# The row vector g_mix of the first norm spread by eight transposes, with V's weights split chunk by chunk

## The chip, the cores and the metric

The kernel runs on one NeuronCore of one Trainium2 chip. The metric is the device time of one execution in microseconds (us); lower is better. A core has five engines that run their own instruction streams in order and wait for each other through semaphores: TensorE (PE, with its weight loads listed apart as PEld), VectorE (DVE), ScalarE (ACT), GpSimd (POOL) and SyncE (SP), from which most transfers are issued.

## The reference

One layer of an encoder for 512 positions (rows) of 1024 values. Cut to what matters here:

```python
def rms_norm(x, g):
    y = x * lax.rsqrt(jnp.mean(jnp.square(x), axis=-1, keepdims=True) + 1e-6)
    return y * g

u = rms_norm(x, g_mix)                 # x: 512 x 1024, g_mix: 1024
z = u @ w_in                           # w_in: 1024 x 4360; columns q, k, v of two branches, f, gates
y_a = sliding_window_attention(q_a, k_a, v_a, sinks) @ w_br_swa
y_b = forgetting_attention(q_b, k_b, v_b, f_b + b_forget) @ w_br_fox
g0, g1 = sigmoid(gate_logits)
h = x + (g0 * y_a + g1 * y_b) @ w_mix_out
h = h + square(relu(rms_norm(h, g_mlp) @ w_ff1)) @ w_ff2
h = h + sigmoid(rms_norm(h, g_ple) @ w_ple_gate) * (p @ w_ple_proj)
out = rms_norm(h, g_final)
```

The change concerns the first two lines alone: the first norm, and the product of its result with the 648 columns of w_in that hold V of both branches and the forget logits.

## The kernel before

**Tiling.** The 512 rows are four blocks of 128 (`tb` 0 to 3), the 1024 columns eight chunks of 128 (`k` 0 to 7). Every product is made three times with operands cut in a high and a low part: ACT writes the high part (a cast), DVE the low one (the difference), and PE adds high x high, high x low and low x high.

**The first stage (lines 403 to 520).** For a block `tb`, `square1` (lines 432 and 439 on ACT, 435 on DVE for block 0's second half) makes sums of squares, `rms_rstd` (lines 359 and 362, POOL) the reciprocal root `n_rs`, and `scale1` (line 447, DVE) two scaled halves `n_xn` of 128 x 512, multiplied by `g_bc`, the vector g_mix repeated on all 128 partitions. `to_uT` transposes the eight chunks on PE (line 379, `n_tr`, four chunks to a PSUM tile), and `hi_lo` cuts them in `u` high (line 70, ACT) and low (line 71, DVE). `split_v(k)` cuts the chunk's rows of V's weights, `wv`, into `wv_h` (line 452, ACT) and `wv_l` (line 453, DVE). `v_mm(tb, k, nk)` (line 466) takes the chunks into the two accumulators `va` and `vb`: for nk chunks first u high x wv_h, then u high x wv_l, then u low x wv_h, each as a pair of matmuls of 320 and 328 columns.

**Where g_bc comes from.** `g_row` is loaded as one row on one partition; two matmuls with a row of ones (line 494) repeat it on all partitions in two PSUM tiles `g_ps`, and ACT copies them to `g_bc` (line 501). PE runs 16 transposes of the identity before (line 490, `warm`) and 14 behind (line 498), whose results nobody reads.

**The order.** In this stage the order on PE, POOL, ACT, DVE and SP is the one in which the code is written (`manual_schedule`). Block 0: scale, `split_v` 0 and 1, both halves of `to_uT`, `split_v` 2 and 3, `v_mm` of the chunk pairs 0-1 and 2-3, squares of block 1, `split_v` 4 and 5, scale of block 1, `split_v` 6 and 7, `v_mm` 4-5, transposes of block 1, `v_mm` 6-7. Blocks 1 to 3 follow chunk by chunk.

**The transfers.** SP issues them in the order x block 0 (two halves, `g_row` between them), `wv` for chunks 0-1 and 2-3, x block 1, `wv` 4-5, `wv` 6-7, x blocks 2 and 3. `wv` has three buffers, so that `wv` 6-7 is issued when DVE has done `wv_l` of chunk 1.

Of the kernel before, what the change touches and what calls it, by code (L numbers as in the profile page):

```python
# [8 lines left out]
F32 = mybir.dt.float32  # L9
# [5 lines left out]
P = 128  # L15
S = 512
D = 1024
NT = S // P
KT = D // P
# [4 lines left out]
EPS = 1e-6  # L24
C_QA, C_KA, C_VA, C_QB, C_KB, C_VB, C_F, C_G = 0, 512, 640, 768, 1280, 1792, 2304, 2312

N_WARM = 16
N_WARM2 = 14
N_PIECES = 4
N_PRE = 4  # L30
SWA_ACT = (0, 1)
# [19 lines left out]
def layer_kernel(ctx: ExitStack, tc: tile.TileContext, x, p, g_mix, w_in, b_forget, swa_sinks,  # L51
# [318 lines left out]
                                           ALU.mult)  # L370
        return xn

    def to_uT(xn, uh, ul, tb, trp, name, tg="tr"):

        for half in range(2):
            tr = trp.tile([P, 4, P], F32, tag=tg, bufs=3, name=f"{name}_tr{half}")
            for j in range(4):
                k = half * 4 + j
                nc.tensor.transpose(tr[:, j, :], xn[:, k * P:(k + 1) * P], ident)
            sl = (slice(None), slice(half * 4, half * 4 + 4), slice(tb * P, (tb + 1) * P))  # L380
            hi_lo(uh[sl], ul[sl], tr)
# [21 lines left out]
    s0_st = ExitStack()  # L403
    s0 = s0_st.enter_context(tc.tile_pool(name="s0", bufs=1))
    g_bc = s0.tile([P, D], F32, name="g_mix_bc")
    g_row = s0.tile([1, D], F32, name="g_row")
    ones_row = s0.tile([1, P], F32, name="ones_row")
    nc.vector.memset(ones_row, 1.0)
    wv_h = s0.tile([P, KT, 648], F32R, name="wv_h")
    wv_l = s0.tile([P, KT, 648], F32R, name="wv_l")  # L410
    xts, wvs, xn1 = [], [], {}
# [1 line left out]
    def load_x(tb):  # L413
        xt = s0.tile([P, D], F32, tag="xt", bufs=3, name=f"x_{tb}")
        for half in range(2):
            if tb == 0 and half == 1:
                nc.sync.dma_start(g_row, g_mix)
            sl = slice(half * 512, half * 512 + 512)
            nc.sync.dma_start(xt[:, sl], x[tb * P:(tb + 1) * P, sl])
        xts.append(xt)  # L420

    def load_wv(k):
# [6 lines left out]
    def square1(tb):  # L429
        acc = sm.tile([P, 2], F32, tag="acc1", name=f"acc1_{tb}")  # L430
        xn = xn1[tb] = s0.tile([P, D], F32, tag="xn", bufs=2, name=f"n1_{tb}_xn")
        nc.scalar.activation(xn[:, 0:512], xts[tb][:, 0:512], AF.Square, scale=1.0 / 32,
                             accum_out=acc[:, 0:1])
        if tb == 0:
            nc.vector.tensor_tensor_reduce(out=xn[:, 512:], in0=xts[tb][:, 512:],
                                           in1=xts[tb][:, 512:], scale=1.0 / D, scalar=0.0,
                                           op0=ALU.mult, op1=ALU.add, accum_out=acc[:, 1:2])
        else:
            nc.scalar.activation(xn[:, 512:], xts[tb][:, 512:], AF.Square, scale=1.0 / 32,
                                 accum_out=acc[:, 1:2])  # L440
        return acc

    def scale1(tb, acc):
        rs = rms_rstd(acc, f"n1_{tb}")
        for half in range(2):
            sl = slice(half * 512, half * 512 + 512)
            nc.vector.scalar_tensor_tensor(xn1[tb][:, sl], xts[tb][:, sl], rs, g_bc[:, sl],
                                           ALU.mult, ALU.mult)

    def split_v(k):  # L450
# [24 lines left out]

    with tc.manual_schedule(engines={ET.Activation, ET.DVE, ET.SP}):
        load_x(0)
        load_wv(0)
        load_wv(2)
        load_x(1)  # L480
        load_wv(4)
        load_wv(6)
        load_x(2)
        load_x(3)
        bcast_row(bf_bc, b_forget[0])
        bcast_row(sink_bc, swa_sinks[0])

        warm = psA.tile([P, 4, P], F32, tag="tr", bufs=3, name="warm")
        for j in range(N_WARM):
            nc.tensor.transpose(warm[:, j % 4, :], ident, ident)  # L490
        gps = []
        for half in range(2):
            ps = psA.tile([P, S], F32, tag="sc", bufs=3, name=f"g_ps{half}")
            nc.tensor.matmul(ps, ones_row, g_row[:, half * 512:half * 512 + 512], start=True,
                             stop=True)
            gps.append(ps)
        for j in range(N_WARM2):
            nc.tensor.transpose(warm[:, j % 4, :], ident, ident)
        acc = square1(0)
        for half in range(2):  # L500
            nc.scalar.copy(g_bc[:, half * 512:half * 512 + 512], gps[half])
        scale1(0, acc)
        split_v(0)
        split_v(1)
        to_uT(xn1[0], uh, ul, 0, psA, "n1_0")
        split_v(2)
        split_v(3)
        v_mm(0, 0, 2)
        v_mm(0, 2, 2)
        acc = square1(1)  # L510
        split_v(4)
        split_v(5)
        scale1(1, acc)
        split_v(6)
        split_v(7)
        v_mm(0, 4, 2)
        to_uT(xn1[1], uh, ul, 1, psA, "n1_1")
        v_mm(0, 6, 2)
        for tb in range(1, NT):
            if tb < NT - 1:  # L520
                acc = square1(tb + 1)
                scale1(tb + 1, acc)
            v_out(tb - 1)
            for k in range(KT):
                v_mm(tb, k)
                if k == 4 and tb < NT - 1:
                    to_uT(xn1[tb + 1], uh, ul, tb + 1, psA, f"n1_{tb + 1}")
            if tb == 2:
                unit("ka")
        v_out(NT - 1)  # L530
# [948 lines left out]
```

## Time and profile before

| | |
|---|---|
| median of 3 runs | 721.81 us (720.74 to 724.39) |
| the profiled execution | 720.46 us, of which the span from first to last instruction is 718.7 us |
| granted TensorE clock, mean | 0.995 |
| PE / DVE / ACT busy | 706.7 us (98%) / 530.8 us (74%) / 449.8 us (63%) |
| the first V matmul | starts at 10.10 us |

A row of the timeline gives the start in us from the start of the span, the time taken in us, the engine, the line, the operation, the tiles written and read, the count of instructions that were merged in the row, and in brackets how long the engine was idle before it and what ended that. Matmuls overlap, so that a single PE row is longer than the distance to the next one.

### The profile page before, as it was taken

Reading aid. Unit: us, or ns where it says so; the run is one execution under the profiler, and the core shown is the slowest. Engines: PE = TensorE matmul, PEld = TensorE weight load, DVE = VectorE, ACT = ScalarE, POOL = GpSimd, SP = SyncE. Lnnn points to the kernel's source line nnn. Section 1 sums busy time; section 2 is a strip of 40 time slices with the busy share of each in tenths; the row PEclk is TensorE's granted clock in tenths of the full one; section 3 lists DMA queues with packets and bytes.
Section 4 is the critical chain, followed back from the end, with each engine's and each line's share of the span. In section 5 each row is a group of like instructions: output and inputs, shape, how many; then the busy total and the mean of one; then the engine's idle time right before and its main releaser. Section 6 shows DMA issues by size and latency. Waiting matters only on the chain.

```text
span 718.7 us, 11465 instructions
## 1 busy us (share of the span) xinstructions
PE 706.7 (98%) x4234; PEld 627.1 (87%) x4234; DVE 530.8 (74%) x898; ACT 449.8 (63%) x838; POOL 86.5 (12%) x127
## 2 busy tenths in 40 slices
PE   9999999999999999999999999999999999999995
PEld 7988888888888998888899889988999899988884
DVE  6557888877696556545879985899579966997564
ACT  6547888779853553344777636874578546866452
POOL 1011211100001200002410102010300020010101
PEclk9999999999999999999999999999999999999998
DMA  9256456670364894450995599749995689079002
GB/s 279 76 163 159 116 123 157 153 192 1 118 210 112 157 347 153 159 174 8 256 216 203 107 287 171 232 87 262 184 255 117 159 231 227 31 147 352 0 30 88
DMA packets 74041, 116.72 MB, mean 162 GB/s; under 512 B 6657, under 2 KB 44033, under 8 KB 73986
## 3 DMA queue, kind: packets, MB, share of 16 engines
q1 hardware_dynamic: 65922, 86.64, 38.1%
q0 software_dynamic: 8064, 29.36, 22.1%
q8 instruction: 33, 0.54, 0.3%
q14 instruction: 22, 0.18, 0.1%
HBM read 72.93 MB, written 4.19 MB: 107 GB/s over the span
## 4 chain that ended last, share of the span: by engine, by line
PE 89%; DVE 6%; ACT 2%; DMA 1%; issue 1%; POOL 0%; POOLq 0%; DVEq 0%; ACTq 0%
PE pf L74 5%; PE pf L76 5%; PE pf L75 5%; PE s_6x L1295 3%; PE s_4x L1295 3%; PE s_2x L1295 3%; PE s_0x L1295 3%; PE h_sc L738 2%; PE h_pv L808 2%; PE h_tr L796 2%; PE psm L76 2%; PE psm L74 2%; PE psy L74 2%; PE psy L75 2%; PE psm L75 2%; PE psy L76 2%
## 5 line engine op out<-in xcount | busy, mean ns | idle before, releaser
L298 POOL DMA_DIRECT2D wq<-wq x26 | 23.6, 943 | 173.5 <-DVE u154l L325 25.9
L756 ACT ACTIVATE s<-s,h_nm 128x128 f32<-128x128 f32 (+1 forms) x64 | 32.6, 512 | 5.9 <-DVE h_nm L749 5.2
L71 DVE TENSOR_TENSOR h_ptl<-h_tr,h_pth 128x512 fp32r<-128x512 f32 (+2 forms) x40 | 22.9, 604 | 4.0 <-ACT h_pth L70 3.6
L359 POOL TENSOR_SCALAR n_ms<-acc 128x1 f32<-128x1 f32 x15 | 5.2, 344 | 165.3 <-ACT junk L1061 100.3
L70 ACT CAST h_pth<-h_tr 128x512 fp32r<-128x512 f32 (+2 forms) x40 | 19.5, 523 | 1.8 <-PE h_tr L796 1.4
L70 ACT CAST u<-n_tr 128x512 fp32r<-128x512 f32 x22 | 12.1, 585 | 13.1 <-PE n_tr L1109 5.8
L466 PE MATMUL va<-wv_h,u 128*128 128x320 f32 x64 | 19.9, 316 | 0.2 <-ACT u L70 0.2
L796 PE MATMUL h_tr<-ident,s 128*128 128x128 f32 x136 | 19.6, 277 | 0.2
L466 PE MATMUL vb<-wv_h,u 128*128 128x328 f32 x64 | 19.5, 313 | 0.0
L298 POOL DMA_DIRECT2D wgw<-wgw x8 | 7.1, 971 | 101.7 <-DVE u25l L325 77.7
L71 DVE TENSOR_TENSOR u<-n_tr,u 128x512 fp32r<-128x512 f32 x22 | 14.5, 684 | 6.2 <-ACT u L70 6.2
L1061 ACT ACTIVATE junk<-h_sb 128x512 f32<-128x512 f32 x16 | 10.1, 630 | 12.3 <-DVE h_sb L1051 9.8
L808 PE MATMUL h_pv<-h_ptl,v 128*128 128x256 f32 (+1 forms) x64 | 16.9, 305 | 0.4 <-DVE h_ptl L71 0.3
L808 PE MATMUL h_pv<-h_pth,v 128*128 128x256 f32 (+1 forms) x64 | 17.3, 291 | 0.0
L796 PEld LDWEIGHTS h_tr<-ident,s 128*128 128x128 f32 x136 | 15.0, 141 | 2.0 <-ACT s L776 0.5
L1385 DVE TENSOR_TENSOR sgp<-sgp,pp 128x512 f32<-128x512 f32 (+1 forms) x9 | 5.7, 633 | 14.8 <-ACT sgp L1384 14.8
L1051 DVE TENSOR_TENSOR h_sb<-psm,h_sb 128x512 f32<-128x512 f32 x8 | 5.5, 689 | 14.3 <-PE psm L76 14.3
L776 ACT ACTIVATE s<-s,h_rec 128x128 f32<-128x128 f32 (+2 forms) x32 | 14.2, 482 | 2.4 <-DVE h_rec L770 2.4
L818 DVE TENSOR_TENSOR h_ao<-h_pv,h_ao 64x512 f32<-64x512 f32 x16 | 10.9, 681 | 6.0 <-ACT h_ao L817 5.8
L744 DVE CUSTOM_DVE_ANT_0 s<-h_sc,causal 128x128 f32<-128x128 f32 (+3 forms) x32 | 13.8, 483 | 0.3 <-PE h_sc L738 0.3
L770 DVE RECIPROCAL h_rec<-h_den 128x4 f32<-128x4 f32 x16 | 3.0, 185 | 14.5 <-ACT s L756 14.3
L808 PEld LDWEIGHTS h_pv<-h_ptl,v 128*128 128x128 f32 x64 | 12.1, 188 | 1.7 <-DVE h_ptl L71 0.8
(1606 smaller groups left out, 2775.4 us busy)
## 6 DMA issues: line engine op xcount, KB each, us to landing
wq<-in_w_ff_dram SPq DMA_DIRECT2D x45, 512.0 KB, 4.9
wq<-wq POOLq DMA_DIRECT2D x26, 512.0 KB, 5.5
wq_c<-in_w_ff_dram SPq DMA_DIRECT2D x9, 512.0 KB, 6.0
wg<-in_w_in_dram SPq DMA_DIRECT2D x4, 1024.0 KB, 5.3
wgw<-in_w_in_dram SPq DMA_DIRECT2D x8, 512.0 KB, 4.8
wgw<-wgw POOLq DMA_DIRECT2D x8, 512.0 KB, 5.8
wmix<-in_w_mix_out_dram SPq DMA_DIRECT2D x4, 1024.0 KB, 5.1
wpg<-in_w_ple_gate_dram SPq DMA_DIRECT2D x4, 1024.0 KB, 8.4
```

The source lines that it names most:

```text
L70: nc.scalar.copy(hi, src)
L71: nc.vector.tensor_tensor(lo, src, hi.bitcast(F32), ALU.subtract)
L74: nc.tensor.matmul(ps, lh, rh, start=start, stop=False)
L75: nc.tensor.matmul(ps, lh, rl, start=False, stop=False)
L76: nc.tensor.matmul(ps, ll, rh, start=False, stop=stop)
L298: nc.gpsimd.dma_start(q, other, accum_op=ALU.add)
L466: nc.tensor.matmul(ps, u[:, kk_, ts_], w[:, kk_, c0:c1], start=kk_ == 0 and n == 0, stop=kk_ == KT - 1 and n == 2)
L738: nc.tensor.matmul(ps[:, off:off + n], qs[i][z][:, qb * P:(qb + 1) * P], kk[i][z][:, k0:k0 + n], start=z == 0, stop=z == 1)
L756: nc.scalar.activation(sl, sl, AF.Exp, bias=nm[:, qb:qb + 1], accum_out=den[:, qb:qb + 1])
L796: nc.tensor.transpose(tr[:, n, :], c["s"][:, o, :], ident)
L808: nc.tensor.matmul(pv[:, q0:q0 + nq, :], V2[kb][:, c["v"], :], t[:, o:o + nq, :], start=n == 0, stop=n == 2 * NT - 1, skip_group_check=True)
L1295: nc.tensor.matmul(ps, o[:, j, ts_], w[:, j, :], start=tg != "" and j == 0 and n == 0, stop=j == 1 and n == 2, skip_group_check=True)
```

## The change

`g_row` is loaded as 8 rows of 128 instead of 1 row of 1024, and one transpose turns it into 8 columns `g_col`, which DVE copies out of PSUM. Eight transposes, each of one column read 128 times, then fill the two PSUM tiles `g_ps`. Block 0's scaling reads these PSUM tiles, and the copies to `g_bc` stand behind it. The idle transposes number 10, 4 and 6 in three places. The second half of x block 0 is issued by ACT. In block 0, `split_v` goes chunk by chunk, `to_uT` in two halves with V matmuls between, `v_mm` takes one chunk at a time, and the scaling of block 1 stands ahead of `split_v` 4 to 7.

```diff
-N_WARM = 16
-N_WARM2 = 14
+N_WARM = (10, 4, 6)
...
-    def to_uT(xn, uh, ul, tb, trp, name, tg="tr"):
+    def to_uT(xn, uh, ul, tb, trp, name, tg="tr", halves=(0, 1)):
-        for half in range(2):
+        for half in halves:
...
-    g_row = s0.tile([1, D], F32, name="g_row")
-    ones_row = s0.tile([1, P], F32, name="ones_row")
-    nc.vector.memset(ones_row, 1.0)
+    g_row = s0.tile([KT, P], F32, name="g_row")
+    g_col = s0.tile([P, KT], F32, name="g_col")
...
-            if tb == 0 and half == 1:
-                nc.sync.dma_start(g_row, g_mix)
             sl = slice(half * 512, half * 512 + 512)
-            nc.sync.dma_start(xt[:, sl], x[tb * P:(tb + 1) * P, sl])
+            queue = nc.scalar if tb == 0 and half == 1 else nc.sync
+            queue.dma_start(xt[:, sl], x[tb * P:(tb + 1) * P, sl])
+            if tb == 0 and half == 0:
+                nc.sync.dma_start(g_row, g_mix[0].rearrange("(k q) -> k q", q=P))
...
-            nc.vector.scalar_tensor_tensor(xn1[tb][:, sl], xts[tb][:, sl], rs, g_bc[:, sl],
+            nc.vector.scalar_tensor_tensor(xn1[tb][:, sl], xts[tb][:, sl], rs,
+                                           gps[half] if tb == 0 else g_bc[:, sl],
                                            ALU.mult, ALU.mult)
...
-        for j in range(N_WARM):
-            nc.tensor.transpose(warm[:, j % 4, :], ident, ident)
+        def warm_up(n):
+            for j in range(n):
+                nc.tensor.transpose(warm[:, j % 4, :], ident, ident)
+        warm_up(N_WARM[0])
+        ps = psA.tile([P, KT], F32, tag="mm", bufs=2, name="g_colps")
+        nc.tensor.transpose(ps, g_row, ident[0:KT, 0:KT])
+        nc.vector.tensor_copy(g_col, ps)
+        warm_up(N_WARM[1])
         gps = []
         for half in range(2):
             ps = psA.tile([P, S], F32, tag="sc", bufs=3, name=f"g_ps{half}")
-            nc.tensor.matmul(ps, ones_row, g_row[:, half * 512:half * 512 + 512], start=True,
-                             stop=True)
+            for j in range(4):
+                k = half * 4 + j
+                nc.tensor.transpose(ps[:, j * P:(j + 1) * P],
+                                    g_col[:, k:k + 1].to_broadcast([P, P]), ident)
             gps.append(ps)
-        for j in range(N_WARM2):
-            nc.tensor.transpose(warm[:, j % 4, :], ident, ident)
+        warm_up(N_WARM[2])
         acc = square1(0)
+        scale1(0, acc)
         for half in range(2):
             nc.scalar.copy(g_bc[:, half * 512:half * 512 + 512], gps[half])
-        scale1(0, acc)
         split_v(0)
-        split_v(1)
-        to_uT(xn1[0], uh, ul, 0, psA, "n1_0")
-        split_v(2)
-        split_v(3)
-        v_mm(0, 0, 2)
-        v_mm(0, 2, 2)
+        to_uT(xn1[0], uh, ul, 0, psA, "n1_0", halves=(0,))
+        v_mm(0, 0)
+        for k in (1, 2, 3):
+            split_v(k)
+            if k == 1:
+                v_mm(0, 1)
+        to_uT(xn1[0], uh, ul, 0, psA, "n1_0", halves=(1,))
+        v_mm(0, 2)
+        v_mm(0, 3)
         acc = square1(1)
-        split_v(4)
-        split_v(5)
         scale1(1, acc)
-        split_v(6)
-        split_v(7)
-        v_mm(0, 4, 2)
+        for k in range(4, KT):
+            split_v(k)
+        v_mm(0, 4)
+        v_mm(0, 5)
         to_uT(xn1[1], uh, ul, 1, psA, "n1_1")
-        v_mm(0, 6, 2)
+        v_mm(0, 6)
+        v_mm(0, 7)
```

Three places show how the order on the engines changes; behind V of block 0 it is the same in both programs.

On DVE, the stretch from block 0's scaling to the low parts of chunks 4 and 5, before (`n_0_xn` and `n_1_xn` are the scaled blocks 0 and 1; `wv_109`, `wv_112`, `wv_118`, `wv_121` hold chunks 0-1, 2-3, 4-5 and 6-7):

```order
L447 SCALAR_TENSOR_TENSOR n_0_xn<-x_105,n_0_rs,g_mix_bc 128x512 x2
L453 TENSOR_TENSOR wv_l<-wv_109,wv_h 128x648 x2
L71 TENSOR_TENSOR u_80<-n_0_tr_183,u_80 128x4x128
L71 TENSOR_TENSOR u_80<-n_0_tr_190,u_80 128x4x128
L453 TENSOR_TENSOR wv_l<-wv_112,wv_h 128x648 x2
L453 TENSOR_TENSOR wv_l<-wv_118,wv_h 128x648 x2
L447 SCALAR_TENSOR_TENSOR n_1_xn<-x_115,n_1_rs,g_mix_bc 128x512 x2
L453 TENSOR_TENSOR wv_l<-wv_121,wv_h 128x648 x2
```

The same stretch of DVE after (`wv_108`, `wv_111`, `wv_117`, `wv_120` are the same four weight tiles; the program's lines are one to thirteen higher):

```order
L447 SCALAR_TENSOR_TENSOR n_0_xn<-x_104,n_0_rs,g_ps_149 128x512
L447 SCALAR_TENSOR_TENSOR n_0_xn<-x_104,n_0_rs,g_ps_154 128x512
L454 TENSOR_TENSOR wv_l<-wv_108,wv_h 128x648
L71 TENSOR_TENSOR u_80<-n_0_tr_179,u_80 128x4x128
L454 TENSOR_TENSOR wv_l<-wv_108,wv_h 128x648
L454 TENSOR_TENSOR wv_l<-wv_111,wv_h 128x648 x2
L71 TENSOR_TENSOR u_80<-n_0_tr_206,u_80 128x4x128
L447 SCALAR_TENSOR_TENSOR n_1_xn<-x_114,n_1_rs,g_mix_bc 128x512 x2
L454 TENSOR_TENSOR wv_l<-wv_117,wv_h 128x648 x2
L454 TENSOR_TENSOR wv_l<-wv_120,wv_h 128x648 x2
```

Block 1's scaling has moved ahead of the low parts of chunks 4 and 5, and the second half's `u` low behind those of chunks 2 and 3.

On ACT, the same stretch before, with what each instruction waits for in brackets (a wait that names an engine is for a result or a finished read of that engine):

```order
L501 COPY g_mix_bc<-g_ps_149 128x512 [waits PE_49]
L501 COPY g_mix_bc<-g_ps_151 128x512 [waits PE_49]
L452 CAST wv_h<-wv_109 128x648 [waits DMAHW4_49,DMAHW3_49]
L452 CAST wv_h<-wv_109 128x648
L70 CAST u_80<-n_0_tr_183 128x4x128 [waits PE_49]
L70 CAST u_80<-n_0_tr_190 128x4x128 [waits PE_49]
L452 CAST wv_h<-wv_112 128x648 [waits DMAHW6_49,DMAHW5_49]
L452 CAST wv_h<-wv_112 128x648
L432 ACTIVATE n_1_xn,acc_1_227<-x_115 128x512 [waits DMAHW7_49]
```

And ACT after:

```order
L512 COPY g_mix_bc<-g_ps_149 128x512 [waits DVE_49]
L512 COPY g_mix_bc<-g_ps_154 128x512 [waits DVE_49]
L453 CAST wv_h<-wv_108 128x648 [waits DMAHW4_49,DMAHW3_49]
L70 CAST u_80<-n_0_tr_179 128x4x128 [waits PE_49]
L453 CAST wv_h<-wv_108 128x648
L453 CAST wv_h<-wv_111 128x648 [waits DMAHW6_49,DMAHW5_49]
L453 CAST wv_h<-wv_111 128x648
L70 CAST u_80<-n_0_tr_206 128x4x128 [waits PE_49]
L432 ACTIVATE n_1_xn,acc_1_225<-x_114 128x512 [waits DMAHW7_49]
```

The two copies of `g_ps` wait for DVE, which now reads these tiles first, and no longer for PE; the second half's `u` high has moved behind the casts of chunks 1 to 3, and block 1's squares stay behind it.

On PE, where block 0's second half is transposed, before (`n_0_tr_190` is that half's PSUM tile, `va_201` and `vb_202` the accumulators):

```order
L379 MATMUL n_0_tr_183<-ident,n_0_xn 128x128 x4
L379 MATMUL n_0_tr_190<-ident,n_0_xn 128x128 x4
L466 MATMUL va_201<-wv_h,u_80 128x320
L466 MATMUL vb_202<-wv_h,u_80 128x328
L466 MATMUL va_201<-wv_h,u_80 128x320
```

And after, the end of chunk 1 and what follows (`n_0_tr_206` is the second half's tile, `va_186` and `vb_187` the accumulators):

```order
L467 MATMUL va_186<-wv_l,u_80 128x320 [waits DVE_49]
L467 MATMUL vb_187<-wv_l,u_80 128x328
L467 MATMUL va_186<-wv_h,u_80 128x320
L467 MATMUL vb_187<-wv_h,u_80 128x328
L379 MATMUL n_0_tr_206<-ident,n_0_xn 128x128 x4
L467 MATMUL va_186<-wv_h,u_80 128x320 [waits Activation_49]
```

The transposes of the second half now stand behind all V matmuls of chunks 0 and 1, the last of which wait for DVE's `wv_l` of chunk 1.

## The prediction

> **What bounds the kernel now.** I read first who waits on PE in the whole run (us in total, times, longest), then the busy time by stretches (start:end, length, then busy us and rows of each engine):
>
> ```profile
> PE warm L490 <- POOL ident masks.py:199: 1.4, 1, 1.4
> PE ('f1', 0)x L896 <- ACT u_('f1', 0)_4205 L907: 0.5, 1, 0.5
> PE h_pv L808 <- DVE h_ptl L71: 0.3, 1, 0.3
> PE va L466 <- ACT u L70: 0.2, 1, 0.2
> 0.00:50.00 50.00, 48.23 (x292) 44.14 (x293) 31.30 (x79) 28.35 (x69) 7.52 (x21) 1.00 0.55 170
> 50.00:100.00 50.00, 49.41 (x278) 42.22 (x277) 37.92 (x129) 37.84 (x115) 8.73 (x13) 1.00 0.59 148
> 350.00:400.00 50.00, 49.47 (x384) 47.47 (x383) 41.70 (x47) 40.05 (x59) 8.82 (x10) 1.00 0.83 216
> ```
>
> PE is the bound: it is idle 1.8 us in the first 50, and no more than 0.6 us in any of the two later stretches. So whatever the first stage gains or loses reaches the end nearly whole; only waits in later stretches, 0.5 us and less each, could take a bit of it up. The question is when PE gets through V of block 0.
>
> Next comes the timeline of the start, up to the first V matmul:
>
> ```profile
> 1.42 3.67 PE L490 MATMUL warm<-ident 128*128 128x128 f32 x16 [1.42 <-POOL ident masks.py:199]
> 3.44 0.63 ACT L432 ACTIVATE n_xn<-x 128x512 f32<-128x512 f32 x1 [1.37 <-DMA x<-in_x_dram]
> 5.02 2.28 PE L494 MATMUL g_ps<-g_row,ones_row 1*128 1x512 f32 x4
> 5.09 0.69 DVE L435 CUSTOM_DVE_ANT_0 n_xn<-x 128x512 f32<-128x512 f32 x1 [4.02 <-DMA x<-in_x_dram]
> 6.36 0.57 POOL L362 TENSOR_TENSOR n_rs<-n_ms,mhalf 128x1 f32<-128x1 f32 x1
> 7.17 1.54 DVE L447 SCALAR_TENSOR_TENSOR n_xn<-x,n_rs,g_mix_bc 128x512 f32<-128x512 f32 x2 [1.38 <-POOL n_rs L362]
> 7.24 1.75 PE L498 MATMUL warm<-ident 128*128 128x128 f32 x14
> 7.34 0.59 ACT L501 COPY g_mix_bc<-g_ps 128x512 f32<-128x512 f32 x1 [0.27 <-PE g_ps L494]
> 7.82 1.37 ACT L452 CAST wv_h<-wv 128x648 fp32r<-128x648 f32 x2
> 8.63 1.57 DVE L453 TENSOR_TENSOR wv_l<-wv,wv_h 128x648 fp32r<-128x648 f32 x2
> 8.82 1.04 PE L379 MATMUL n_tr<-ident,n_xn 128*128 128x128 f32 x8
> 9.46 1.08 ACT L70 CAST u<-n_tr 128x512 fp32r<-128x512 f32 x2 [0.27 <-PE n_tr L379]
> 10.10 0.42 PE L466 MATMUL va<-wv_h,u 128*128 128x320 f32 x1 [0.24 <-ACT u L70]
> 10.12 1.28 DVE L71 TENSOR_TENSOR u<-n_tr,u 128x512 fp32r<-128x512 f32 x2
> ```
>
> The scaling starts at 7.17, when POOL has n_rs, which waited for x's second half (5.09). Its first half is done by 7.92, but the transposes start only at 8.82, since the two outer products and 14 idle transposes stand before them on PE. There the change sees its gain. But ACT and DVE have no gap from 7.2 on, and that goes on behind:
>
> ```profile
> 11.69 0.64 ACT L432 ACTIVATE n_xn<-x 128x512 f32<-128x512 f32 x1
> 12.32 0.62 ACT L439 ACTIVATE n_xn<-x 128x512 f32<-128x512 f32 x1
> 13.52 0.57 POOL L362 TENSOR_TENSOR n_rs<-n_ms,mhalf 128x1 f32<-128x1 f32 x1
> 13.69 1.58 DVE L453 TENSOR_TENSOR wv_l<-wv,wv_h 128x648 fp32r<-128x648 f32 x2 [0.81 <-ACT wv_h L452]
> 14.78 1.37 ACT L452 CAST wv_h<-wv 128x648 fp32r<-128x648 f32 x2 [0.49 <-DMA wv<-in_w_in_dram]
> 15.18 1.41 DVE L447 SCALAR_TENSOR_TENSOR n_xn<-x,n_rs,g_mix_bc 128x512 f32<-128x512 f32 x2
> 15.32 0.42 PE L466 MATMUL va<-wv_l,u 128*128 128x320 f32 x1
> 16.33 1.03 PE L379 MATMUL n_tr<-ident,n_xn 128*128 128x128 f32 x8
> 16.51 1.57 DVE L453 TENSOR_TENSOR wv_l<-wv,wv_h 128x648 fp32r<-128x648 f32 x2
> ```
>
> Chunks 4 and 5 get their low parts at 13.69, before block 1's scaling at 15.18, and PE follows closely (15.32); block 1's transposes start at 16.33. That start is my milestone: from there PE has the same instructions in both programs.
>
> **The change part by part.** I call S the start of block 0's scaling and work out the rest from it.
>
> Start of the scaling. x's second half moves to ACT's queue, and g_row stays behind the first half on SP's:
>
> ```profile
> 0.80 0.39 SPq L419 DMA_DIRECT2D x<-in_x_dram  x1
> 1.60 0.36 SPq L419 DMA_DIRECT2D x<-in_x_dram  x1
> 2.00:3.00 1.00, 1.00 (x7) 1.00 (x6) 0.00 (x0) 0.07 (x1) 0.00 (x0) 1.00 0.76 262
> 3.00:4.00 1.00, 1.00 (x6) 1.00 (x5) 0.00 (x0) 0.56 (x2) 0.00 (x0) 1.00 0.83 215
> ```
>
> The second half can be issued 0.8 us earlier, but the transfer engines were already 0.76 to 0.83 busy between 2 and 4 us (last but one number of the row). The two halves share them: both 256 KB at 215 to 262 GB/s from about 2.1 arrive near 4.3, the first half later than its 3.4, the second earlier than 5.1, and g_row behind the first half near 4.3 too. Then come g_row's transpose (by the 0.23 us distance of the first 16 to the 0.42 of a single matmul), DVE's copy of 128 x 8, and only behind it, on the same engine, the squares of the second half. The nearest row to that copy:
>
> ```profile
> 22.97 0.15 DVE L474 TENSOR_TENSOR fl<-vb,bf_bc 128x8 f32<-128x8 f32 x1
> ```
>
> So the squares start near 4.6 instead of 5.09, and S is 6.7. Bounds: 6.4 if x and g_row come by 3.9, 7.2 if DVE stands as late as now. ACT's table load moves 0.4 behind its issue and still ends before x is there. The Trainium skill ("Trainium Kernel Development and Optimization", Key Constraints) speaks against this part: transfers issued from several engines interleave on the same 16 engines, and a second issuer saves issue time alone. By it the gain is at most the 0.8 us of issue; the shares of 0.76 and 0.83 agree, and S stays within the bounds.
>
> The eight transposes and 6 idle ones: 14 at 0.125 (row at 7.24) to 0.23 us (row at 1.42) from about 4.8 end at 6.6 to 8.0; reading one column 128 times has no row here, and these two distances are its bounds. Block 0's first transposes need the scaled half at S + 0.75 = 7.45; what ACT does next, below, covers all of this up to 8.6. The scaling reads g from PSUM: between 0 and 0.1 us more, inside the bounds of S.
>
> ACT. The copies of g_ps now wait for DVE's read of the same tile. That such reads go one after the other, the trace shows: ACT's cast of `vb` stood still until DVE's read of it was done.
>
> ```profile
> 22.08 0.35 DVE L71 TENSOR_TENSOR v<-vb,v 128x192 fp32r<-128x192 f32 x1
> 22.46 0.27 ACT L70 CAST v<-vb 128x128 fp32r<-128x128 f32 x1 [2.63 <-DVE v L71]
> ```
>
> So the second copy starts when both halves are scaled, S + 1.57, and the next instruction 0.48 later (7.34 to 7.82): wv_h of chunk 0 at S + 2.05 = 8.75 (now 7.82). Casts stand 0.64 apart: `u` high of the first half at 9.39, done at 9.93, and the **first V matmul at 10.0 instead of 10.10**. What PE's shorter start saves, ACT's longer one takes. Casts of chunks 1 to 3 follow until 11.8.
>
> DVE. wv_l 0 starts when its cast is done, 8.75 + 0.77 = 9.52; `u` low 0.75 later, at 10.27; wv_l of chunk 1 another 0.6 later, at 10.87, done at 11.70. PE needs it before chunk 1's last two pairs of matmuls (a pair is 0.3 us) and these before the second half's transposes: these start at 12.35, and ACT can cut them from 12.98 to 13.46, though it was free from 11.8. wv 6-7 is issued 1.5 us later than now (10.2 to 11.7) and lands as much later, near 16.2; DVE reaches it at 19, which hides that.
>
> Block 1's norm, the term that decides. Its squares stand behind that cut on ACT, so start at 13.46 instead of 11.69. Now from there to n_rs on DVE are 2.64 us (13.52 + 0.57, and 0.24 as between 6.93 and 7.17, from 11.69): 16.10. **DVE stands still until then**, with wv_l 4 to 7 queued behind the scaling, though wv_h 4 is cast by 15.4. Two halves take 1.33 (15.18 to 16.51): wv_l 4 starts at 17.43 instead of 13.69, PE has it at 18.3. Ten matmuls of chunks 4 and 5 (0.15 each) lead to block 1's transposes at 19.8 instead of 16.33: 3.5 us later. Behind that nothing is late: wv_l 5 to 7 follow 0.75 apart, while PE takes 0.9 for a chunk. Now PE loses some 0.1 us there, since wv_l 6 and 7 come late (16.51, two in 1.57); that goes.
>
> Sum: **+3.4 us**, between +3.1 and +3.9 by the bounds of S. If the copies did not hold up ACT, wv_h of chunk 0 could start 1.1 us earlier, as now at 7.8 when its weights are there, and the sum would be about 2.3. On the profiled execution, 720.46 (span 718.7, and 1.8 around it), that is 723.9; the median of the runs shown, 721.81, lies 1.35 higher, and my forecast for the median is 721.81 + 3.4 = 725.2, 0.47% over.
>
> **The rivals.** (1) The gap costs clock. Chunks 2 and 3 need no more than the first half's cut and wv_l 3, and PE ends them near 14.6; chunk 4's first pair waits for its cast (15.4) and ends at 15.9; then PE stands until 18.3. That is 0.3 us of work in 3.7, and 2.4 without any. The first 16 transposes took 0.23 us each, the 14 at 7.24 took 0.125: PE starts at half speed and rises some 4 us after it began, without a trace of it in the granted clock (1.00 in both windows). If the gap lets it fall back, up to 4 us run at half speed: 2.0 us more, +5.4, 727.2. For it: PE idles longer than anywhere now. Against it: each part of the gap is shorter than the time that the rise took. The Trainium skill ("TensorE: Matmul & The Clock Gate", Part 1) puts the fall behind an idle window of about 3.4 us; by that rule 2.4 us do not reach it, 3.7 with one pair inside might, and no row of this profile shows it.
>
> (2) Not slower: the loss is absorbed further back. The mechanism is a stage that waits for transfers paced by themselves; the chain that ended last has one such piece of length:
>
> ```profile
> 362.20 5.97 DMA wq<-wq
> ```
>
> If that piece sets the time whatever PE does before, up to 3.4 us vanish there and the time is 721.8 or, where the first stage still gains, just below. It decides if PE stood still there by at least as much; but PE is idle 0.53 us in 350 to 400 (row above), and the transfers there are issued behind DVE's results, which shift along.
>
> (3) The change does what it is built for: first V matmul well ahead of 10.10 and block 0 in time. Ahead of block 1's scaling everything would have to be 3.4 us earlier, an S of 3.3, which is before x is there (3.44). By the order shown it cannot be; it stays as the chance that I misread a wait. Its price: from 10.10 to 16.33 PE has 36 matmuls at 0.15, 5.4 of 6.2 us; the 0.8 of waits between them would go, and with 721.81 that is 721.0.
>
> **How the numbers follow.** Forecast, +2.3 to +4.1: 0.72; rival 1: 0.16; rival 2: 0.08; rival 3: 0.04. The predicted time is the likeliest case's, 725.2. The range runs from the profiled execution plus 2.3, less 0.4 for what later waits may take up, 722.4, to the median plus rival 1's 5.4, 727.2; it leaves out rivals 2 and 3. About what a measurement of this kernel can tell from no change is 0.5%, 3.6 us. That lies inside the forecast's own band, of which I put three eighths above it (0.27). With rival 1, slower is 0.43; the rest of the forecast (0.45), rival 2 and half of rival 3 make 0.55; faster is 0.02.
>
> **What would show it.** Right: first V matmul within 0.5 of 10.0; DVE idle before block 1's scaling until about 16, released by n_rs; PE idle for 2 to 3 us before a `va<-wv_l` released by DVE; block 1's transposes near 19.8, all later stages shifted alike. Rival 1: matmuls behind the gap at 0.3 us apart. Wrong would be a PE that passes block 1's transposes before 18, an ACT copy of g_ps that starts before the scaling ends, or a last stage that is not later though the first is.

## The result and the profile after

After: **725.59 us**, median of 21 runs (723.82 to 727.05). Before, on the same chip: 722.29, median of 21 runs (719.92 to 725.74). The ratio is 1.0037, with a 95% interval of 1.0022 to 1.0052: the changed kernel takes 0.37% longer. The profiled execution took 723.82 us with a span of 721.8, against 720.46 and 718.7 before.

The waits of PE, the same view as the first one in the prediction (us in total, times, longest):

```profile
PE va L467 <- DVE wv_l L454: 2.1, 1, 2.1
PE va L467 <- ACT wv_h L453: 0.7, 1, 0.7
PE va L467 <- ACT u L70: 0.7, 1, 0.7
PE g_colps L497 <- DMA g_row<-in_g_mix_dram: 0.5, 1, 0.5
```

All four are new, or larger than before, and all stand in the first 20 us. The busy time by stretches, with the columns of the prediction:

```profile
0.00:50.00 50.00, 44.62 (x273) 42.13 (x274) 28.88 (x69) 26.06 (x63) 7.24 (x21) 1.00 0.55 170
50.00:100.00 50.00, 49.43 (x276) 42.12 (x276) 37.22 (x127) 37.78 (x116) 8.98 (x14) 1.00 0.57 143
350.00:400.00 50.00, 49.44 (x386) 47.40 (x385) 41.42 (x47) 38.75 (x59) 9.67 (x10) 1.00 0.84 224
```

PE's busy time falls from 48.23 to 44.62 us in the first stretch, and the two later ones are as they were (49.41 and 49.47 before). So it all happens in the first stage. Its timeline after, up to the first V matmul:

```profile
1.42 2.40 PE L494 MATMUL warm<-ident 128*128 128x128 f32 x10 [1.42 <-POOL ident masks.py:199]
4.30 0.27 PE L497 MATMUL g_colps<-ident,g_row 8*128 8x8 f32 x1 [0.49 <-DMA g_row<-in_g_mix_dram]
4.50 1.11 PE L494 MATMUL warm<-ident 128*128 128x128 f32 x4
5.41 1.92 PE L505 MATMUL g_ps<-ident,g_col 128*128 128x128 f32 x8
6.69 1.42 DVE L447 SCALAR_TENSOR_TENSOR n_xn<-x,n_rs,g_ps 128x512 f32<-128x512 f32 x2 [1.31 <-POOL n_rs L362]
7.12 1.49 PE L494 MATMUL warm<-ident 128*128 128x128 f32 x6
7.47 1.26 ACT L512 COPY g_mix_bc<-g_ps 128x512 f32<-128x512 f32 x2 [2.59 <-DVE n_xn L447]
8.40 1.06 PE L379 MATMUL n_tr<-ident,n_xn 128*128 128x128 f32 x4
8.62 0.73 ACT L453 CAST wv_h<-wv 128x648 fp32r<-128x648 f32 x1
10.13 0.42 PE L467 MATMUL va<-wv_h,u 128*128 128x320 f32 x1 [0.68 <-ACT u L70]
```

The scaling starts 0.48 us earlier than before (6.69 against 7.17), but the first V matmul stands where it stood (10.13 against 10.10). The eight transposes of g take 0.24 us each (length of the row over the count), the idle ones behind them 0.25. The second half of the first stage:

```profile
12.33 0.60 PE L379 MATMUL n_tr<-ident,n_xn 128*128 128x128 f32 x4
12.97 0.59 ACT L70 CAST u<-n_tr 128x512 fp32r<-128x512 f32 x1 [0.99 <-PE n_tr L379]
13.45 0.64 ACT L432 ACTIVATE n_xn<-x 128x512 f32<-128x512 f32 x1
15.46 0.41 PE L467 MATMUL va<-wv_h,u 128*128 128x320 f32 x1 [0.74 <-ACT wv_h L453]
15.87 1.41 DVE L447 SCALAR_TENSOR_TENSOR n_xn<-x,n_rs,g_mix_bc 128x512 f32<-128x512 f32 x2 [1.59 <-POOL n_rs L362]
17.20 3.06 DVE L454 TENSOR_TENSOR wv_l<-wv,wv_h 128x648 fp32r<-128x648 f32 x4
18.08 0.41 PE L467 MATMUL va<-wv_l,u 128*128 128x320 f32 x1 [2.05 <-DVE wv_l L454]
19.67 1.03 PE L379 MATMUL n_tr<-ident,n_xn 128*128 128x128 f32 x8
```

Read it from the bottom up: block 1's transposes (19.67, before 16.33) follow V of chunk 4, which waits 2.05 us for its low part; that comes behind block 1's scaling on DVE, and this waits 1.59 us for n_rs, whose squares (13.45) stand on ACT behind the cut of the second half. Whether those 3.34 us reach the end is seen at the first transposes behind the last norm that has any, in the timelines of before and of after:

```profile
659.88 1.04 PE L379 MATMUL n_tr<-ident,h_sb 128*128 128x128 f32 x8
662.96 1.04 PE L379 MATMUL n_tr<-ident,h_sb 128*128 128x128 f32 x8
```

They do, but for 0.26 us: 3.08 later. So these two profiles agree with each other. The medians ask for more, for the times of both kernels come in **two groups**. Over the four series of timed runs in this study, before has 52 of 96 times from 719.9 to 722.4 (median 721.2) and 44 from 723.9 to 727.0 (median 724.6), with none in between (two single runs outside these series, 722.58 and 723.00, do lie there); after has 9 of 33 up to 724.62 (median 724.3) and 24 from 725.46 on (median 725.9). Both profiles above are of the lower groups. What the groups are is a second question for the experiments.

### The profile page after: what moved, and what is told of

Its sections match the earlier page's. It is cut to its first block, busy times and chain, and to the rows that moved or that the text cites. A ratio compares the mean times of both kernels' runs of the same rounds, so it can differ in the third digit from the quotient of the medians.

```text
span 721.8 us, 11454 instructions
## 1 busy us (share of the span) xinstructions
PE 706.2 (98%) x4229; PEld 627.8 (87%) x4229; DVE 530.9 (74%) x898; ACT 449.8 (62%) x838; POOL 86.3 (12%) x127
## 4 chain that ended last, share of the span: by engine, by line
PE 89%; DVE 6%; ACT 2%; DMA 1%; issue 1%; POOL 0%; POOLq 0%; DVEq 0%; SPq 0%; ACTq 0%
PE pf L74 5%; PE pf L76 5%; PE pf L75 5%; PE s_6x L1308 3%; PE s_2x L1308 3%; PE s_4x L1308 3%; PE s_0x L1308 3%; PE h_sc L751 2%; PE h_pv L821 2%; PE h_tr L809 2%; PE psm L75 2%; PE psm L76 2%; PE psy L75 2%; PE psm L74 2%; PE psy L76 2%; PE psy L74 2%
## 5 line engine op out<-in xcount | busy, mean ns | idle before, releaser
L809 PE MATMUL h_tr<-ident,s 128*128 128x128 f32 x136 | 19.6, 277 | 0.2
L467 PE MATMUL vb<-wv_h,u 128*128 128x328 f32 x64 | 19.6, 312 | 0.0
L1074 ACT ACTIVATE junk<-h_sb 128x512 f32<-128x512 f32 x16 | 10.1, 630 | 12.4 <-DVE h_sb L1064 9.8
L467 PEld LDWEIGHTS va<-wv_h,u 128*128 128x128 f32 x64 | 12.0, 188 | 2.2 <-ACT u L70 1.1
```

The costliest lines, as they stand in the source:

```text
L467: nc.tensor.matmul(ps, u[:, kk_, ts_], w[:, kk_, c0:c1], start=kk_ == 0 and n == 0, stop=kk_ == KT - 1 and n == 2)
L809: nc.tensor.transpose(tr[:, n, :], c["s"][:, o, :], ident)
```

## The experiments

Every kernel is edited from the changed one. "Milestone" is the start of block 1's transposes, as in the prediction. A kernel given without a ratio was run once.

**1. Which part of the order costs the 3.3 us.** Four kernels on one chip; before took 722.10 there (median of 35).

*late_scale*: block 1's scaling back where it was among the splits.

```diff
         acc = square1(1)
+        split_v(4)
+        split_v(5)
         scale1(1, acc)
-        for k in range(4, KT):
-            split_v(k)
+        split_v(6)
+        split_v(7)
```

> The changed kernel with block 1's scaling put back behind split_v 4 and 5 (as before the change). Milestone: start of block 1's transposes, 16.33 us before the change, 19.67 after. Theory 'order' (DVE stands still for block 1's scaling with wv_l 4 to 7 queued behind it): wv_l 4 starts when its cast is done, near 15.5 instead of 17.20, the milestone comes to 17.7, and the whole is about 1.9 us shorter than the changed kernel, some +1.4 us on the kernel before. Rival 'front' (the new way of spreading g and the second half of x on ACT's queue cost the time): milestone stays near 19.7. Rival 'clock' (the gap on PE loses the TensorE clock): the gap is smaller by the same 1.9, so milestone near 17.7 but more than 1.9 us regained at the end.

Measured 722.69 (722.33 to 723.79, 12 runs), ratio 0.9997 (0.9979 to 1.0014), milestone 18.06 (17.7 was expected). It regains 1.6 of the 3.34 us. Its median lies 1.6 us under the changed kernel's lower group (724.3), but 2.9 under that kernel's median (725.59): more than the milestone accounts for, which is what the rival 'clock' had said. Chunk 4's low part now waits only for its own cast:

```profile
15.59 1.58 DVE L454 TENSOR_TENSOR wv_l<-wv,wv_h 128x648 fp32r<-128x648 f32 x2 [1.16 <-ACT wv_h L453]
18.06 1.20 PE L379 MATMUL n_tr<-ident,n_xn 128*128 128x128 f32 x8
```

*both_undone*: late_scale, and block 1's squares ahead of the second half's transposes and cut.

```diff
+        acc = square1(1)
         to_uT(xn1[0], uh, ul, 0, psA, "n1_0", halves=(1,))
         v_mm(0, 2)
         v_mm(0, 3)
-        acc = square1(1)
```

> As the run before, and block 1's squares also ahead of the second half's cut on ACT. Theory 'order': both waits of DVE go; milestone 16.6 to 16.9, only 0.3 to 0.5 us behind the kernel before, and the whole within 0.5 us of it. If the late squares do not matter beside the late scaling, the milestone stays at 17.7. Rival 'front': near 19.7.

Measured 721.55 (721.11 to 722.93, 12 runs), ratio 0.9978 (0.9960 to 0.9995), milestone 16.97: 2.7 us regained by these two orders alone, with the first V matmul still at 10.13. In time too it is 2.7 to 2.8 us under the changed kernel's lower group. Its start is used further below:

```profile
8.20 0.60 PE L379 MATMUL n_tr<-ident,n_xn 128*128 128x128 f32 x4
10.13 0.41 PE L467 MATMUL va<-wv_h,u 128*128 128x320 f32 x1 [1.33 <-ACT u L70]
```

*old_front*: g by outer products and x on one queue as before, with the new order from the first split on. The cut below leaves out the loads, the idle transposes and the operand of the scaling, which are before's as well.

```diff
-                nc.tensor.transpose(ps[:, j * P:(j + 1) * P],
-                                    g_col[:, k:k + 1].to_broadcast([P, P]), ident)
+            nc.tensor.matmul(ps, ones_row, g_row[:, half * 512:half * 512 + 512], start=True,
+                             stop=True)
...
         acc = square1(0)
-        scale1(0, acc)
         for half in range(2):
             nc.scalar.copy(g_bc[:, half * 512:half * 512 + 512], gps[half])
+        scale1(0, acc)
...
```

> The kernel before with its own way to g_bc (outer products, 16 and 14 idle transposes, both halves of x on SP) and only the new order of block 0 from split_v(0) on. Theory 'order': first V matmul near 10.1, milestone 19.6 to 19.8, the whole +3.0 to +3.5 us on the kernel before, as much as the full change. Rival 'front': milestone near 16.3 and no difference from the kernel before.

Measured 726.72 (725.32 to 731.54, 12 runs), ratio 1.0057 (1.0035 to 1.0079): the slowest of the four. From its profile (727.41 us):

```profile
5.02 3.78 PE L494 MATMUL g_ps<-g_row,ones_row 1*128 1x512 f32 x4
13.51 0.42 PE L466 MATMUL va<-wv_h,u 128*128 128x320 f32 x1 [0.68 <-ACT u L70]
21.47 0.41 PE L466 MATMUL va<-wv_l,u 128*128 128x320 f32 x1 [2.06 <-DVE wv_l L453]
23.07 1.03 PE L379 MATMUL n_tr<-ident,n_xn 128*128 128x128 f32 x8
```

From the first V matmul to the milestone are 9.56 us here and 9.54 in the changed kernel: the loss comes with the order, whatever the front. But the first V matmul comes 3.4 us late. The outer products, the same as in before, took 3.78 us instead of 2.28. Neither theory had expected that (19.6 to 19.8 or 16.3 for the milestone).

*old_order*: the new front, with before's order of the work on block 0 and 1.

```diff
         split_v(0)
-        to_uT(xn1[0], uh, ul, 0, psA, "n1_0", halves=(0,))
...
+        split_v(1)
+        to_uT(xn1[0], uh, ul, 0, psA, "n1_0")
+        split_v(2)
+        split_v(3)
+        v_mm(0, 0, 2)
+        v_mm(0, 2, 2)
         acc = square1(1)
+        split_v(4)
+        split_v(5)
         scale1(1, acc)
...
```

> The changed kernel with the old order of block 0 from split_v(0) on; the new spread of g, x's second half on ACT, the copies behind the scaling stay. Theory 'order': scaling starts at 6.7, first V matmul near 10.5, milestone 16.6 to 16.8, the whole +0.3 to +0.5 us on the kernel before: nothing that can be measured. Rival 'front': milestone near 19.7, +3 us.

Measured 721.59 (721.10 to 723.83, 12 runs), ratio 0.9982 (0.9964 to 1.0000), milestone 17.01 (16.6 to 16.8 was expected). That is 0.68 later than in before's profile, yet the median is lower: what it lacks is before's upper group.

**2. ACT's copies, and the gap.** The prediction held that the copies of `g_ps`, which wait for DVE, eat what PE's shorter start saves. Here before took 723.86 (median of 17).

*copies_in_gap*: the two copies moved to ACT's idle 0.99 us ahead of the second half's cut.

```diff
         scale1(0, acc)
-        for half in range(2):
-            nc.scalar.copy(g_bc[:, half * 512:half * 512 + 512], gps[half])
         split_v(0)
...
                 v_mm(0, 1)
+        for half in range(2):
+            nc.scalar.copy(g_bc[:, half * 512:half * 512 + 512], gps[half])
         to_uT(xn1[0], uh, ul, 0, psA, "n1_0", halves=(1,))
```

> The changed kernel with the two copies of g_ps moved on ACT to behind the casts of chunks 1 to 3, where ACT stood idle for 0.99 us. The prediction's step 'ACT takes what PE's shorter start saves' (copies that wait for DVE hold up the first cut): first V matmul 1.1 us earlier (9.0), milestone 18.6. Rival: PE is just as late, since its transposes of g run at 0.23 us and six idle ones stand behind them, and block 0's first transposes end at 9.4 whatever ACT does: first V matmul stays at 10.1, milestone 19.7.

*copies_no_idle*: the same, and without the last six idle transposes.

```diff
-N_WARM = (10, 4, 6)
+N_WARM = (10, 4, 0)
```

> As the run before, and without the last 6 idle transposes. If PE and ACT were late alike: first V matmul near 9.1 to 9.3, milestone 18.8, 0.9 us earlier than in the changed kernel. If only ACT's copies counted: the same as the run before it. If the 6 idle transposes are needed for the clock: V matmuls 0.3 us apart instead of 0.15 for some us and a later milestone.

One run of each: 727.9 and 726.59 us, with milestones of 21.68 and 20.88, later than in the changed kernel (19.67). In both V of chunks 0 and 1 ran at half speed, its matmuls 0.27 us apart instead of 0.15, so only what stands ahead of V can be compared. The start of the first:

```profile
7.08 1.42 DVE L447 SCALAR_TENSOR_TENSOR n_xn<-x,n_rs,g_ps 128x512 f32<-128x512 f32 x2 [1.31 <-POOL n_rs L362]
8.78 1.06 PE L379 MATMUL n_tr<-ident,n_xn 128*128 128x128 f32 x4
10.52 0.64 PE L467 MATMUL va<-wv_h,u 128*128 128x320 f32 x1 [0.68 <-ACT u L70]
```

The first V matmul stands 3.44 us behind the start of the scaling, exactly as in the changed kernel (10.13 - 6.69). Without the copies nothing is gained here, because block 0's transposes can't start earlier: PE is still in its idle transposes until 8.78. Without these as well they start at 7.89 and the first V matmul at 9.68, 0.84 earlier, though later than the 9.1 to 9.3 expected. So two conditions of equal length stood side by side. That holds where PE is still slow at 8.3 us, as in this run and in the changed kernel's profile. In both_undone and late_scale, which have the copies where the changed kernel has them, PE was at full speed by then and done with these transposes by 8.9; it then stood idle for 1.33 and 1.15 us until ACT's cut, and the first V matmul came at 10.13 and 10.06 all the same. There the copies alone set it. No run takes only the copies out of such an execution.

*squares_first*: block 1's squares ahead of the second half's cut, with the scaling left where the change put it (the edit is the one of both_undone without late_scale's).

> The changed kernel with block 1's squares ahead of the second half's cut on ACT and nothing else. Theory 'order', with the two waits adding up: n_rs of block 1 comes 1.6 us earlier, the milestone (start of block 1's transposes, 19.67 in the changed kernel) at 18.1. If the squares wait for something else, it stays at 19.7.

One run: 724.27 us, milestone 19.55, hardly less than 19.67. But V of chunks 0 and 1 ran at half speed again, and the second half's transposes came at 13.79 instead of 12.33. POOL's last step to n_rs does start earlier, at 13.95 instead of 15.27. The scaling starts only at 15.77 even so, behind DVE's cut of the second half (15.16), which had to wait for those late transposes. Less their 1.46 us the milestone would be 18.1, an estimate and not a measurement. By it each of the two orders is worth about 1.6 alone (late_scale for the other), and both together 2.7.

*gap_filled*: 16 idle transposes into the gap, ahead of V of chunk 4; nothing reads their result.

```diff
+        fill = psA.tile([P, 4, P], F32, tag="tr", bufs=3, name="fill")
+        for j in range(16):
+            nc.tensor.transpose(fill[:, j % 4, :], ident, ident)
         v_mm(0, 4)
         v_mm(0, 5)
```

> The changed kernel with 16 idle transposes on PE ahead of chunk 4's V matmuls, so that PE runs in most of its gap of 3.7 us. Theory 'order': milestone 19.7 and the whole the same as the changed kernel within 0.5 us. Rival 'clock' (the gap loses the TensorE clock in some executions, though not in the profiled one): the whole up to 2 us shorter than the changed kernel.

Measured 724.69 (724.10 to 726.22, 12 runs), ratio 1.0018 (1.0002 to 1.0035). Eleven of the 12 times lie between 724.1 and 725.3. The twelfth is the profiled one, which began with V at half speed as squares_first did; so its milestone, 21.33, can't be set beside 19.67. The idle transposes leave PE 1.30 us of waiting for `wv_l`. The upper group of the changed kernel is gone, on the same chip on which copies_in_gap and copies_no_idle were run.

**3. What the two groups are.** Another chip; before took 721.75 there (median of 23).

*after_again*: the changed kernel once more, so as to get a profile from its upper group. *before_again* and *before_third* (on yet another chip): before once more, for the same reason.

> The changed kernel once more, timed on the same chip as the others of this set. Theory 'clock falls in the gap' (PE's gap of 3.7 us, if it covers one of the clock's windows, costs some 3.4 us at half speed, 1.7 us): times in two groups about 1.7 us apart, near 724.2 and 725.9. Otherwise one group.

> The kernel before once more, with a trace. Theory 'late clock': if the time is near 724.5, the two outer products take 3.8 us instead of 2.28 and the first V matmul starts near 13.5 instead of 10.10; if it is near 721, the trace is as the one known, with a rise of the clock at 5.9.

> The kernel before a third time, with a trace; 44 of its 96 timed executions so far lie in a group near 724.6, 3.4 us above the other near 721.2. Theory 'late clock': if this execution falls in the upper group, its two outer products take about 3.8 us as in the run with the old front and the new order, the scaling's second half waits for ACT's second copy of g, and the first V matmul starts near 13.5; block 1's transposes near 19.8. If it falls in the lower group, the first V matmul starts near 10.1 to 10.6 and the theory rests on that other run.

after_again took 725.88 (723.85 to 727.21, 12 runs), ratio 1.0041 (1.0024 to 1.0058), and its profile, of a run of 725.63 us, is of the upper group. PE's rows behind the gap, then the stretches around it (start:end, length, PE's busy us and rows, granted clock, DMA share, GB/s):

```profile
18.27 0.41 PE L467 MATMUL va<-wv_l,u 128*128 128x320 f32 x1 [2.06 <-DVE wv_l L454]
...
19.14 0.47 PE L467 MATMUL vb<-wv_h,u 128*128 128x328 f32 x1
19.41 0.47 PE L467 MATMUL va<-wv_l,u 128*128 128x320 f32 x1
...
20.49 1.91 PE L379 MATMUL n_tr<-ident,n_xn 128*128 128x128 f32 x8
...
22.47 0.32 PE L467 MATMUL vb<-wv_h,u 128*128 128x328 f32 x1
```

```profile
10.00:18.00 8.00, 5.34 (x30) 1.00 0.90 264
18.00:20.00 2.00, 1.73 (x9) 0.76 0.97 262
20.00:23.00 3.00, 3.00 (x16) 0.59 1.11 346
23.00:25.00 2.00, 2.00 (x15) 1.00 0.35 106
```

Behind the gap the clock is at half for a while: matmuls 0.27 us apart, the eight transposes 1.91 us instead of 1.03, and the granted clock 0.76 and 0.59 in two of these stretches, where the first profile of the changed kernel has 1.00 in both. From 19.2 to 22.4 us it reads 0.50. The two rows make 0.96 and 2.46 us at half, so from about 19.0 to 22.5: 3.4 us that cost 1.7. This is the prediction's rival 1. It can be seen without a profile too: each run lists its mean granted clock, and all 9 runs of the lower group have 0.996, all 24 of the upper 0.993 to 0.995. The copies_in_gap and copies_no_idle profiles have the fall as well (0.67 from 20 to 23 us in the one, 0.50 in the other).

before_again, 722.58 us, lies between the groups by its time; its start is that of the first profile of before (outer products 1.98 us, first V matmul 10.58), with the milestone at 16.98. There V's first weights are cast at 8.68, behind a wait of 1.27 us for their transfer, instead of at 7.82. before_third, 724.37 us, was of the upper group, and it begins as old_front did:

```profile
5.02 3.78 PE L494 MATMUL g_ps<-g_row,ones_row 1*128 1x512 f32 x4
7.82 0.75 DVE L447 SCALAR_TENSOR_TENSOR n_xn<-x,n_rs,g_mix_bc 128x512 f32<-128x512 f32 x1 [1.95 <-POOL n_rs L362]
8.73 3.25 PE L498 MATMUL warm<-ident 128*128 128x128 f32 x14
8.84 0.59 ACT L501 COPY g_mix_bc<-g_ps 128x512 f32<-128x512 f32 x1 [1.12 <-PE g_ps L494]
9.46 0.75 DVE L447 SCALAR_TENSOR_TENSOR n_xn<-x,n_rs,g_mix_bc 128x512 f32<-128x512 f32 x1 [0.89 <-ACT g_mix_bc L501]
11.77 1.92 PE L379 MATMUL n_tr<-ident,n_xn 128*128 128x128 f32 x8
13.51 0.64 PE L466 MATMUL va<-wv_h,u 128*128 128x320 f32 x1
20.10 1.05 PE L379 MATMUL n_tr<-ident,n_xn 128*128 128x128 f32 x8
```

Against the rows of before in the prediction: outer products 3.78 instead of 2.28 us, 14 idle transposes 3.25 instead of 1.75, block 0's transposes at 11.77 instead of 8.82, and the first V matmul at 13.51 instead of 10.10. TensorE here reaches full speed only behind 14 us, where the first profile had it by 6. In this start the outer products hold up the copies, the second copy the second half of the scaling, and the idle transposes those of block 0. It is the one profile there is from before's upper group.

**4. The good half of the change.** *mixed*, in the third group of runs: the new spread of g and x on two queues, V's splits chunk by chunk; but both halves of block 0 are transposed ahead of V, the squares and scaling of block 1 stand where before had them, the copies of `g_ps` behind chunk 5's split, and the last idle transposes are left out.

```diff
-N_WARM = (10, 4, 6)
+N_WARM = (10, 4, 0)
...
-        for half in range(2):
-            nc.scalar.copy(g_bc[:, half * 512:half * 512 + 512], gps[half])
         split_v(0)
         to_uT(xn1[0], uh, ul, 0, psA, "n1_0", halves=(0,))
...
+        split_v(1)
         to_uT(xn1[0], uh, ul, 0, psA, "n1_0", halves=(1,))
...
         acc = square1(1)
+        split_v(4)
+        split_v(5)
+        for half in range(2):
+            nc.scalar.copy(g_bc[:, half * 512:half * 512 + 512], gps[half])
         scale1(1, acc)
...
```

> The changed kernel's way to spread g, x's second half on ACT and V matmuls chunk by chunk, but: both halves of to_uT ahead of the V matmuls of chunk 0, block 1's squares and scaling where they stood before the change, the copies of g_ps on ACT behind split_v 5 (where ACT waits for weights), and no idle transposes behind those of g. Theory 'order' (ACT's and DVE's order in block 0 sets the time): first V matmul 9.1 to 9.5, milestone (start of block 1's transposes) 15.8 to 16.1 against 16.33 before the change and 19.67 after. Theory 'late clock' (the kernel before loses 3.5 us in those of its executions in which TensorE's clock rises late, since its scaling waits for two long outer products; the new spread does not): times in one group, 720 to 721, about 0.3% under the median of the kernel before. Without it: two groups 3.5 us apart, as the kernel before.

Measured **720.97** (720.61 to 721.66, 12 runs), ratio 0.9975 (0.9958 to 0.9993): faster than both kernels by little, and in one group. The first V matmul comes at 8.93, but the milestone at 17.13, not earlier than in before_again (16.98, same chip); the expected milestone was missed. There the weights of chunks 4 and 5 hold it:

```profile
13.87 1.37 ACT L453 CAST wv_h<-wv 128x648 fp32r<-128x648 f32 x2 [0.79 <-DMA wv<-in_w_in_dram]
14.64 1.58 DVE L454 TENSOR_TENSOR wv_l<-wv,wv_h 128x648 fp32r<-128x648 f32 x2 [1.82 <-ACT wv_h L453]
```

So in this profile an earlier first block gains nothing beyond the weights' landing. The gain of mixed is that it has no upper group: its median lies with before's lower one (721.2).

## Why the prediction came out as it did

**The order of block 0: right, step by step.**

| step | forecast | measured |
|---|---|---|
| S, start of block 0's scaling | 6.7 | 6.69 |
| first V matmul | 10.0 | 10.13 |
| transposes of the second half | 12.35 | 12.33 |
| ACT's cut of them | 12.98 | 12.97 |
| block 1's squares | 13.46 | 13.45 |
| n_rs on DVE | 16.10 | 15.87 |
| `wv_l` 4 | 17.43 | 17.20 |
| PE has it | 18.3 | 18.08 |
| milestone | 19.8 | 19.67 |

The largest deviation, 0.23 us, is in the way from the squares to n_rs. The sum was +3.4; the two profiles differ by 3.36 us in time and 3.1 in span. The two orders named as its cause give back 2.7 of it together (both_undone). The rest, some 0.6 us, is no more than before itself varies: its milestone stands at 16.33 in one profile and at 16.98 in before_again, where both_undone (16.97) and old_order (17.01) have theirs.

**ACT's copies: half wrong.** "What PE's shorter start saves, ACT's longer one takes" named one of two conditions. The 14 transposes on PE were bounded at 6.6 to 8.0; they ended at 8.40, since they all ran at the slower distance and the eight started at 5.41 rather than near 4.8. The forecast had put at nothing the four idle transposes ahead of the eight, which PE runs from 4.50 to 5.41. So PE was as late as ACT in this execution, and "if the copies did not hold up ACT ... the sum would be about 2.3" was wrong for it: with PE this slow the first V matmul stays where it is (copies_in_gap). Where PE reached full speed by 8.3 us, the step was right as written (both_undone, late_scale). The number survived since both ways led to the same 10.1.

**Rival 1 came true, in most runs.** The clock does fall in the gap: 24 of 33 times, at 1.6 us each by the groups' medians (725.9 - 724.3). It had a chance of 0.16 and a price of 2.0. The argument against it, that each part of the gap is shorter than the rise, failed: 0.74 us of idle time, one pair of matmuls and 2.06 us of idle time count together. gap_filled shows that it hangs on the gap: filled, no time of the upper kind is left but the one with the slow start, whose granted clock is 0.998, while both runs on that chip that keep the whole gap (copies_in_gap, copies_no_idle) have the fall. The Trainium skill ("TensorE: Matmul & The Clock Gate", Part 1) has the gate watch a free-running window of about 3.4 us; that the fall comes in one execution and not in the next agrees with a window whose start is free, though the profile doesn't show the window, and a stretch with a pair of matmuls in it suffices here.

**What I hadn't seen: before has such a term too.** I took the spread of before's three times (720.74 to 724.39) as noise around one program. It was two groups, 3.4 us apart (724.6 - 721.2), and before_third shows the late rise of the clock as the cause in one execution of the upper one. By the times it hits before in 44 of 96 runs. The profile of old_front, which has before's front, shows it too. The kernels with the new front and without the gap (late_scale, both_undone, old_order, mixed) show no upper group in 48 runs; the highest are single times of 723.83 and 723.79. At a share of 44 in 96 chance would hardly do that. Yet the new front is not immune: in the four profiles of the second group of runs V of chunk 0 ran at half speed. Its price there is smaller, some 1.6 us: gap_filled's profiled run took 726.22 us, the median of its other eleven is 724.65. That no outer products stand in front of V there fits this, but no run separates it.

**The account.** Like against like, the lower groups differ by 724.3 - 721.2 = +3.1; of these both_undone gives back 2.7 to 2.8. The fall adds 1.6 x 24/33 = +1.2 on average; before's own late rise takes off 3.4 x 44/96 = 1.6. Together +2.7, as the means have it (725.57 over 33 runs, 722.87 over 96). This splits the means up and is no test of its own; the tests are the profiles and gap_filled. So 725.2 was near 725.59 because the largest term was right, and by luck in the rest: two smaller terms, one with too low a chance and one not seen, nearly cancel, and its base, 721.81, was the median of three times out of both groups of before.

**Rivals 2 and 3 fell.** The transposes behind the last norm come 3.08 us later: nothing on the way took the loss up. The other profiles say the same. In the 11 without a fall of the clock, these transposes stand 643.3 to 644.1 us behind the milestone in ten, whether it is at 16.33 or at 23.07, and 645.0 in before_again. And the change didn't bring block 0 ahead. Where it gained a microsecond (mixed, 8.93), the weights' landing took it back.

## What to carry to other kernels

When a step is put first in the code, look at what its input waits for on the other engine: block 1's scaling, moved ahead of four ready splits on an in-order engine, made all four wait for an n_rs that was itself queued behind another move. When a bound on one engine is lifted, look for a second one of equal length beside it before pricing the gain. And when a few runs of a kernel lie 3 us apart with none between, take profiles of both kinds before comparing: two kernels may differ in how often they meet a late clock, not only in how long their work takes.

## What the runs showed of the hardware

The clock's rise at the start varies far more than I had thought. PE works from 1.42 us on with few breaks (none over 1.4 us up to 14 us), in every one of these kernels. In mixed g's transposes, at 5.14, already took 0.13 us each (1.04 for eight); in the changed kernel the full speed came between 8.4 and 10.1; in before_third only behind 14. The Trainium skill ("TensorE: Matmul & The Clock Gate", Part 1) speaks of about 3.4 us of sustained work; the 12 us of before_third, of transposes and outer products, don't agree with that as it stands, though in mixed nothing but transposes ran before 5.14. What decides was not found. All four profiles of one chip rose late, but 11 of gap_filled's 12 times on that chip show no such loss, so the chip alone doesn't decide it. The outer products may have a part.

The granted clock shows the fall, but not the slow start. The stretch from 10 to 14 us, of the changed kernel and then of gap_filled, in the columns of above:

```profile
10.00:14.00 4.00, 3.87 (x25) 1.00 0.85 224
10.00:14.00 4.00, 3.54 (x13) 1.00 0.65 129
```

Both have 1.00, yet PE got through 25 instructions in the one and 13 in the other, at nearly the same busy time: V's matmuls were 0.15 and 0.27 us apart, and 0.27 is also their distance behind after_again's gap, where the granted clock does show the fall. At the start of these programs the distance of like instructions tells the clock, and the granted clock doesn't.
